# Recurrence: the third job of each inverse made at step 28 for lines 12 to 19, its masks after the final transposes

## The chip, the cores and the metric

The kernel runs on one core of one Trainium2 chip. A core has TensorE (matrix products into PSUM), VectorE, ScalarE, GpSimd (POOL in the profile) and SyncE (SP, which issues the transfers). The metric is the time of one launch on the device, in microseconds. Before the change the median of three runs is 1203.76 us (1202.25 to 1204.63).

## The reference

One layer of a hybrid backbone for 128 context tokens and 512 latent tokens: an adaptive norm, an input projection, an RWKV-7 branch with 8 heads of 64 that runs forward and backward, a neighbourhood-attention branch, a gated merge, and a feed-forward block. The part that matters here is the recurrence of the RWKV branch, for each direction and head:

```python
def _wkv_step(s, inp):
    r, w, k, v, a, b = inp
    sa = jnp.einsum("bhvk,bhk->bhv", s, a)
    s = s * w[:, :, None, :] + sa[..., None] * b[:, :, None, :] + v[..., None] * k[:, :, None, :]
    return s, jnp.einsum("bhvk,bhk->bhv", s, r)

def _wkv_scan(s0, r, w, k, v, a, b, reverse):
    xs = tuple(jnp.moveaxis(t.astype(jnp.float32), 1, 0) for t in (r, w, k, v, a, b))
    s, ys = lax.scan(_wkv_step, s0.astype(jnp.float32), xs, reverse=reverse)
    return s, jnp.moveaxis(ys, 0, 1)
```

Everything is in float32.

## The kernel before, in words

**Chunks and lines.** The kernel does not step through tokens. It cuts the 640 tokens into ten chunks of 64 and treats two heads at a time, so there are four head pairs, `ct` = 0 to 3, one after the other. A chunk in one direction is a *line*; a head pair has 20 lines, 0 to 9 forward and 10 to 19 backward. Lines 0 to 7 and 12 to 19 belong to the 512 latent tokens, lines 8 to 11 to the 128 context tokens. Within a line the rule "state times a, plus b" makes the 64 tokens depend on each other through a triangular matrix, which has to be inverted; after that the lines are chained by products of 64x64 blocks.

**The stages of a head pair.** `main` makes the triangular matrices N of all lines on TensorE and copies them to `Nt`. `inv` inverts them. `carry` walks the state through the lines, eight steps, and makes the outputs. `out` normalises the outputs of the pair and runs woven into the next pair's `inv`; `prep` makes the operands of the next pair and runs woven into `carry`.

**The inverse.** `inv` transposes `Nt` into `RL` on VectorE (line 1218), with the 32x32 diagonal blocks of all lines side by side, and eliminates in 30 steps `s` = 1 to 30 (lines 1235, 1242, or the pairs of 1249 and 1253), all on VectorE, each step reading the one before. Then come the two final transposes on VectorE, RT (line 1262) and T (line 1264). The off-diagonal 32x32 blocks follow by two groups of 80 small products on TensorE: line 1273 reads RT, its result goes to `Hs` by ScalarE (1278), and line 1287 reads T and `Hs`. The finished inverse is `Rt`: eight copies from T on VectorE (1281), and four copies of the second group's result, two on ScalarE and two on VectorE (1292). `carry` reads `Rt` for the first time in line 1348, and `AG` in line 1321 a little before.

**Jobs and masks.** While VectorE eliminates, TensorE has time, and `inv` puts three *jobs* there, each for a range of lines (`parts8`). A job is `v_job` (lines 0 to 9 only: moves the values to the other half of the partitions and copies them to `ZV` by ScalarE, 1172 and 1178), `t_job` (transposes, 1195, copied to `TG` by ScalarE, 1198) and `g_job`: the products of 1144 and 1147 into three PSUM tiles, and, for lines from 10 up, `flip` (1184), which takes the values of line 19 - l from `ZV` in reversed order. So a backward line needs its forward partner's values in `ZV` first. `g_job` returns a function, the *masks*: four VectorE multiplications (two of 1156 into `AG`, two of 1159 into `TG`) that take the products out of PSUM and zero what lies on the wrong side of the diagonal. `PRM["jobs"]` names the steps of the jobs and `PRM["mds"]` those of the masks, per head pair. Before the change the jobs stand at steps 2, 9 and 16 (2, 11 and 16 in pair 3), for lines 0 to 7, 12 to 19 and 8 to 11, and their masks at steps 4, 11 and 19 (4, 13 and 19).

**PSUM.** Jobs, groups and carry all take PSUM tiles from one rotation of six, tag `w`. A job over lines 12 to 19 takes six of them, and the three of its products are held until its masks are done.

**Order of the work.** The order on TensorE, VectorE, ScalarE and GpSimd is the program's order, written out by hand. `weave` runs a stage's generator and, at each of its yields, pulls a number of *fills* from `fill`, the stream of projection matmuls (128x128 times 128x320, line 196) of the rest of the layer; one entry of `PRM["plan"]` gives the number. Evacuations of the projections, such as the shifts of lines 520 to 523 and the merges of line 1461 (pair 3), are put behind a set number of fills, on ScalarE and VectorE. The plan has ten fills behind each of steps 2, 9 and 16, mostly two behind other steps, and 5, 24 and 20 behind steps 29, 30 and the final transposes in pairs 0 and 1 (18 instead of 20 in pair 2), so that line 1273 stands behind them on TensorE; pair 3 has six behind most steps from 15 on and 11 behind the transposes. The transfers of the weights are issued by SP in the stream's own order. When the fills from the activations `h` end, in pair 3's inverse, the space of `h` is taken over by the attention and recurrence outputs `o`, loaded back from DRAM.

After the four pairs come the merge, the output projection and the feed-forward block, bound by TensorE throughout.

Of the kernel before, what the change touches and what calls it, by code (L numbers as in the profile page):

```python
# [26 lines left out]
PRM = dict(  # L27
    order=("l0 l1 k0 r0 v0 l2 g0 g1 g2 k1 g3 r1 g4 g5 v1 g6 g7 k2 r2 g8 g9 v2 g10 g11 k3 r3 g12 g13 v3 g15 g14 a0 a1 a2 a3 a4 a5 a6 a7 "
     "b0 b1 b2 b4 b3 b5 b6 b7"),
    plan=(  # L30
        "22.0 0.0 2.0 4.0",
        ("0.0.0 2.0.0 2.0.1 10.0.0 2.0.0 2.0.1 2.0.1 2.0.1 2.0.1 2.0.1 10.0.0 2.0.0 2.0.0 10.0.0 2.0.0 2.0.0 "
         "2.0.0 10.0.0 2.0.0 2.0.0 2.0.0 2.0.0 2.0.0 2.0.0 2.0.0 2.0.0 2.0.0 2.0.0 2.0.0 2.0.0 5.0.0 24.0.0 "
         "20.0.0 10.0.0 8.0.0 8.0.0 0.0.0"),
        ("10.0 1.0 12.1 0.2 0.0 8.1 6.2 0.0 8.1 6.2 0.0 8.1 12.2 0.0 8.1 6.2 0.0 8.1 6.2 0.0 7.1 5.2 0.0 9.1 "
# [32 lines left out]
        "w >hb >lb",  # L68
        ""),
    fp=(6, 12, 18), h2e="dpddddpddd", x0e="a", ze="aa", y2=1, y1=0, sc=3, sr=3, sp=1, mg=1.915, h1=0.952,  # L70
    h2=0.91, jobs=((2, 9, 16), (2, 9, 16), (2, 9, 16), (2, 11, 16)),
    mds=((4, 11, 19), (4, 11, 19), (4, 11, 19), (4, 13, 19)), bud=((1.8, 0.8), (1.3, 1.8)), off=6, tk=2, h3=1,
    h4=1.07, g1=2, km="dddddddd", kb="ddpd", ma="d", yo="pppp", r0="pd", rl=(0, 0, 0), lh=(0, 0, 1, 1),
    wl="dddddddddppppppppppppppppppppppppppdpppppppppppp", nu=9, na=(
        "6.0.12.0.1 6.0.12.0.0 6.0.12.0.0 6.0.12.0.2 6.0.12.0.0 6.0.12.0.2 6.0.12.0.0 6.0.12.0.2 6.0.12.0.0 "
        "6.0.12.0.2 6.0.12.1.0 6.1.12.1.2 6.2.12.2.0 6.1.12.2.2 6.0.12.2.0 6.1.12.1.2 6.2.14.2.0 "
        "6.2.14.1.2 6.2.14.2.0 6.2.14.2.0 6.3.18.2.0 10.0.10.0.0"))
# [24 lines left out]
def V(ap, dims, off=0):  # L102

    return bass.AP(ap.tensor, ap.offset + off, [list(ap.ap[0])] + [list(d) for d in dims])
# [3 lines left out]
def body(ctx: ExitStack, tc: tile.TileContext, xs, xp, cols, consts, w_ada, b_row, w_rw, w_qkv,  # L108
# [366 lines left out]
    pend, off, hold = [], [0], [False]  # L475
# [557 lines left out]
    with ExitStack() as s3:  # L1033
# [76 lines left out]
        parts8 = ((0, 8), (12, 20), (8, 12))  # L1110
# [102 lines left out]

        def inv(ct, S):

            jobs, mds = dict(zip(PRM["jobs"][ct], parts8)), PRM["mds"][ct]
            RL = nk_t("RL", [P, 40, 32])[:, :32, :]
            dve.transpose(RL, V(Nt[:, 0, :], [[20, 32], [1, 32]]))

# [5 lines left out]
            masks = []  # L1225
# [36 lines left out]
            dve.transpose(RT, V(RL[:, 0, :], [[1, 32], [32, 32]]))  # L1262
            T = V(f5()[:, :], [[32, 32], [1, 32]])
            dve.transpose(T, RL)
            Hs = nk_t("Hs", [P, 40, 32])
            lohi = [(slice(64 * h, 64 * h + 32), slice(64 * h + 32, 64 * h + 64)) for h in range(2)]
            yield 2
# [223 lines left out]
        with tc.manual_schedule(engines=FIRST):  # L1491
# [4 lines left out]
            for ct in range(4):  # L1496
# [8 lines left out]
                if ct < 3:  # L1505
                    prep_dma(ct + 1, S2, sb.tile([P, NT], F32, tag="mx", bufs=2, name=nm("upw")))
                weave(inv(ct, S), (og, bg))
                drain(og)
                marks.add(f"I{ct}")
# [486 lines left out]
```

## Time and profile before

| what | value |
|---|---|
| median of three runs | 1203.76 us (1202.25 to 1204.63) |
| the profiled execution | 1201.55 us |
| its span, first to last instruction | 1199.8 us |
| mean granted TensorE clock | 0.985 |
| the four pairs' recurrence, about | 262 to 680 us |
| TensorE busy in 262 to 680 us | 381.8 of 418 us |
| VectorE busy in 262 to 680 us | 281.1 of 418 us |

The inverses stand at about 266 to 314, 366 to 420, 470 to 522 and 576 to 638 us of the span, each with the groups behind it. How to read the rows that follow: a row of the timeline is start, duration, engine, line, operation, output and inputs by the program's names, shapes and count, and in brackets the time that the engine sat idle before it and what released it. Several instructions of one line are merged into one row. A row of the chain has start, duration, engine, output and line. PE is TensorE, DVE is VectorE, ACT is ScalarE. Busy time of TensorE includes modelled ends, so a gap shows in the bracket rather than in the share.

### The profile page before, as it was taken

To read this page: it belongs to the slowest core of one execution; us is meant where nothing else is said; L and a number is where in the kernel's file an instruction comes from. 1 tells how busy PE (TensorE), PEld (TensorE's weight loads), DVE (VectorE), ACT (ScalarE), POOL (GpSimd) and SP (SyncE) were. 2 spreads that over 40 slices of the span, in tenths; PEclk is the share of its full clock that TensorE was granted. 3 is DMA by queue.
4 is the path that set the end of the run, shared out by engine and by line. 5 is a ranking of instruction groups with operands and counts; after the bars stand their busy time and mean duration, and the time that the engine had idled before them with its cause. 6 is when DMAs were issued, how large, how long until landed. Compare 5 with 4: busy or idle time off the path is not lost.

```text
span 1199.8 us, 26920 instructions
## 1 busy us (share of the span) xinstructions
PE 1128.0 (94%) x11160; PEld 999.2 (83%) x11160; DVE 793.3 (66%) x1630; ACT 503.6 (42%) x1016; POOL 273.8 (23%) x354
## 2 busy tenths in 40 slices
PE   6999999998998899899789989989999999999998
PEld 4588877788887788788778878889889989998997
DVE  4565455569558838946594684888568756875675
ACT  4444666653454364346323331754224412442240
POOL 1162244343224323342231360200001000000000
PEclk9999999999899999999899989999999999999999
DMA  9752777531211221120432571312312231222122
GB/s 336 245 115 88 238 219 231 197 124 48 66 48 37 83 69 49 54 87 29 164 129 87 177 272 54 105 36 89 106 53 88 89 105 53 89 90 90 67 73 104
DMA packets 56578, 134.48 MB, mean 112 GB/s; under 512 B 7140, under 2 KB 22116, under 8 KB 56456
## 3 DMA queue, kind: packets, MB, share of 16 engines
q1 hardware_dynamic: 55592, 131.56, 33.1%
q8 instruction: 88, 1.44, 0.5%
q10 hardware_dynamic: 864, 1.20, 0.3%
q14 instruction: 34, 0.28, 0.1%
HBM read 118.41 MB, written 14.32 MB: 111 GB/s over the span
## 4 chain that ended last, share of the span: by engine, by line
PE 61%; DVE 11%; issue 2%; ACT 2%; DMA 1%; SPq 0%; POOL 0%; DVEq 0%; ACTq 0%
PE f L1715 23%; PE acc L283 16%; PE fl L196 10%; DVE pr L1249 2%; DVE RL L1253 2%; PE w L1361 1%; PE w L1321 1%; DVE AG L1104 1%; PE w L1333 1%; PE w L1348 1%; PE mm L196 1%; PE w L1147 1%; DMA tr<-trw_d 1%; PE w L1378 1%; DVE f L1262 1%
## 5 line engine op out<-in xcount | busy, mean ns | idle before, releaser
L196 PE MATMUL fl<-h,whi 128*128 128x320 f32 x704 | 170.4, 323 | 1.9 <-ACT U L515 1.0
L175 POOL TENSOR_TENSOR wlo<-wst,whi 128x256 fp32r<-128x256 f32 x118 | 102.8, 899 | 192.1 <-ACT whi L170 188.7
L1715 PE MATMUL f<-t,whi 128*128 128x320 f32 x640 | 141.4, 309 | 0.0
L1715 PE MATMUL f<-b,whi 128*128 128x320 f32 x608 | 136.4, 312 | 3.6 <-ACT b L185 1.8
L283 PE MATMUL acc<-whi,u 128*128 128x512 f32 (+1 forms) x448 | 135.9, 385 | 0.0
L196 PEld LDWEIGHTS fl<-h,whi 128*128 128x128 f32 x704 | 121.1, 192 | 6.8 <-ACT U L515 1.2
L170 ACT CAST whi<-wst 128x1024 fp32r<-128x1024 f32 (+2 forms) x86 | 81.8, 956 | 83.2 <-PE acc L283 32.9
L196 PE MATMUL fl<-h,wlo 128*128 128x320 f32 x352 | 114.6, 326 | 0.0
L1715 PEld LDWEIGHTS f<-t,whi 128*128 128x128 f32 x640 | 107.0, 188 | 0.0
L1715 PEld LDWEIGHTS f<-b,whi 128*128 128x128 f32 x608 | 102.8, 190 | 4.7 <-ACT b L185 2.2
L1770 POOL TENSOR_TENSOR ws<-wst 128x512 f32<-128x512 f32 x20 | 27.4, 1372 | 342.0 <-DVE wlo L1759 226.2
L1715 PE MATMUL f<-t,wlo 128*128 128x320 f32 x320 | 98.9, 309 | 0.0
L283 PEld LDWEIGHTS acc<-whi,u 128*128 128x128 f32 x448 | 83.5, 188 | 16.6
L1715 PE MATMUL f<-b,wlo 128*128 128x320 f32 x304 | 94.6, 311 | 1.4 <-DVE wlo L1759 1.4
L1756 ACT CAST whi<-ws 128x1024 fp32r<-128x1024 f32 x40 | 42.0, 1050 | 108.7 <-PE f L1715 48.5
L283 PE MATMUL acc<-wlo,u 128*128 128x512 f32 (+1 forms) x224 | 86.3, 385 | 0.0
L175 DVE TENSOR_TENSOR wlo<-wst,whi 128x1024 fp32r<-128x1024 f32 (+1 forms) x49 | 61.6, 1267 | 36.5 <-ACT whi L170 36.0
L283 PE MATMUL acc<-whi,h 128*128 128x512 f32 x240 | 78.7, 402 | 1.4 <-DVE h L397 1.4
L196 PEld LDWEIGHTS fl<-h,wlo 128*128 128x128 f32 x352 | 67.8, 193 | 2.6
L1555 DVE SCALAR_TENSOR_TENSOR tt<-acc,G 128x512 f32<-128x512 f32 (+1 forms) x51 | 34.7, 681 | 51.0 <-PE acc L283 51.0
L196 PE MATMUL mm<-h,whi 128*128 128x320 f32 x288 | 65.5, 315 | 0.0
L196 PE MATMUL fl<-o,whi 128*128 128x320 f32 x224 | 56.3, 331 | 7.1 <-DMA o<-o_d 4.8
(332 smaller groups left out, 2562.1 us busy)
## 6 DMA issues: line engine op xcount, KB each, us to landing
wst<-in_w_dram SPq DMA_DIRECT2D x66, 512.0 KB
wst<-in_w_rw_dram SPq DMA_DIRECT2D x31, 512.0 KB
wa<-in_w_ada_dram SPq DMA_DIRECT2D x24, 512.0 KB
f<-in_w_ada_dram SPq DMA_DIRECT2D x16, 512.0 KB
wst<-in_w_qkv_dram SPq DMA_DIRECT2D x12, 512.0 KB
o<-o_d SPq DMA_DIRECT2D x14, 320.0 KB
x<-in_xs_dram SPq DMA_DIRECT2D x8, 512.0 KB
wa<-in_w_ada_dram SPq DMA_DIRECT2D x16, 256.0 KB
```

The costliest lines, as they stand in the source:

```text
L170: act.copy(hi[:, :n], st[:, :n])
L175: eng.tensor_tensor(out=lo[:, a:b], in0=st[:, a:b], in1=hi[:, a:b].bitcast(F32), op=ALU.subtract)
L196: pe.matmul(ps[:, :t1 - t0], w[:, a:a + 128], x[:, k0 + kt, t0:t1], start=n == 0, stop=n == 3 * nk - 1)
L283: pe.matmul(pss[i][:, a:b], lhs(x, kt, ts_), w[:, cs_], start=ki == 0 and n == 0, stop=ki == last and n == 2)
L1104: dve.tensor_tensor(out=AG[rr, c, h, :], in0=c64(S.kk[rr, :], d), in1=S.P65[d][rr, :, 0:64], op=ALU.mult)
L1147: pe.matmul(pr[h][hrows[h ^ i], o_], x[hrows[h], :], R_[hrows[h], l, :], start=True, stop=True)
L1249: dve.tensor_tensor(out=prv, in0=V(RL[:, s + 1 + a, :], [[32, b - a], [0, s]], s), in1=V(RL[:, s, :], [[0, b - a], [1, s]]), op=ALU.mult)
L1253: dve.tensor_tensor(out=dst, in0=dst, in1=prv, op=ALU.add)
L1555: dve.scalar_tensor_tensor(out=tt, in0=ps[:, a:b], scalar=c, in1=G[:, g, sl], op0=ALU.mult, op1=ALU.mult)
L1715: pe.matmul(ps[:, :H2], w_[:, c_], x_[:, kt, :], start=first and kt + n == 0, stop=last and kt == 3 and n == 2, skip_group_check=more)
L1756: act.copy(r[0][:, :width], src())
L1770: eng_x(PRM["se"][i - 1]).tensor_tensor(out=o_, in0=x, in1=y, op=op)
```

## The change

The jobs now stand at steps 2, 9 and 28 (2, 11 and 28 in pair 3). A new parameter `jo` gives their order: the first job is for lines 8 to 11, the second for lines 0 to 7, the third for lines 12 to 19. The masks of the first two follow at steps 4 and 12 (4 and 14); those of the third are made after the two final transposes, ahead of the copies into `Rt`. The numbers of fills in the plan stay as they are.

```diff
-    h2=0.91, jobs=((2, 9, 16), (2, 9, 16), (2, 9, 16), (2, 11, 16)),
-    mds=((4, 11, 19), (4, 11, 19), (4, 11, 19), (4, 13, 19)), bud=((1.8, 0.8), (1.3, 1.8)), off=6, tk=2, h3=1,
+    h2=0.91, jobs=((2, 9, 28), (2, 9, 28), (2, 9, 28), (2, 11, 28)),
+    mds=((4, 12), (4, 12), (4, 12), (4, 14)), bud=((1.8, 0.8), (1.3, 1.8)), off=6, tk=2, h3=1,
...
-    wl="dddddddddppppppppppppppppppppppppppdpppppppppppp", nu=9, na=(
+    wl="dddddddddppppppppppppppppppppppppppdpppppppppppp", nu=9, jo=(2, 0, 1), na=(
...
         def inv(ct, S):
 
-            jobs, mds = dict(zip(PRM["jobs"][ct], parts8)), PRM["mds"][ct]
+            jobs, mds = dict(zip(PRM["jobs"][ct], (parts8[i] for i in PRM["jo"]))), PRM["mds"][ct]
...
             T = V(f5()[:, :], [[32, 32], [1, 32]])
             dve.transpose(T, RL)
+            for f in masks:
+                f()
             Hs = nk_t("Hs", [P, 40, 32])
```

## The prediction

> **What bounds the kernel now.** I read the page first, then the chain that ended last, then the rows of the four inverses by engine. The page gives each engine's busy time and share, and the chain's shares by engine.
>
> ```profile
> PE 1128.0 (94%) x11160; PEld 999.2 (83%) x11160; DVE 793.3 (66%) x1630; ACT 503.6 (42%) x1016; POOL 273.8 (23%) x354
> PE 61%; DVE 11%; issue 2%; ACT 2%; DMA 1%; SPq 0%; POOL 0%; DVEq 0%; ACTq 0%
> ```
>
> TensorE sets the end; the change adds and drops no matmul, so only an idle stretch of TensorE can be won or lost. VectorE holds 11% of the chain, and the chain in order of time (start, duration, work) shows where: at the ends of the inverses. I number these 0 to 3, as `ct`.
>
> ```profile
> 300.27 1.91 DVE f L1262
> 302.32 1.48 PE w L1273 x72
> 303.81 4.34 PE fl L196 x18
> ...
> 309.40 2.83 PE fl L196 x18
> ...
> 410.25 4.06 PE fl L196 x18
> ...
> 512.28 4.08 PE fl L196 x17
> ```
>
> L1262 is the first of the two final transposes (RT), L1273 the matmul group that reads it, L196 the filler projections. TensorE's rows at the group, with the idle time and its releaser in brackets, inverses 0 to 3:
>
> ```profile
> 302.32 1.48 PE L1273 MATMUL w<-f,Nt 32*32 32x32 f32 x80 [5.33 <-DVE f L1262]
> 408.75 1.49 PE L1273 MATMUL w<-f,Nt 32*32 32x32 f32 x80 [3.30 <-DVE f L1262]
> 510.80 1.48 PE L1273 MATMUL w<-f,Nt 32*32 32x32 f32 x80 [3.66 <-DVE f L1262]
> 627.94 1.47 PE L1273 MATMUL w<-f,Nt 32*32 32x32 f32 x80 [0.25 <-DVE f L1262]
> ```
>
> In inverses 0 to 2 TensorE has run out of filler and stands 12.3 us in all for VectorE's elimination. In inverse 3 the two arrive together. After the idles the same 18 fills take 4.34 and 4.06 us where 2.83 is the pace (17: 4.08 against 2.67): 1.51, 1.23 and 1.41 us more, the price of a TensorE that slows after standing.
>
> **The change part by part.** (1) Masks. VectorE's rows of inverse 0 show what a set of masks costs in its queue: from its first row to the elimination step behind it.
>
> ```profile
> 280.53 1.39 DVE L1156 TENSOR_TENSOR AG<-w,K 64x512 f32<-64x512 f32 x2
> ...
> 283.04 0.57 DVE L1249 TENSOR_TENSOR pr<-RL 128x108 f32<-128x108 f32 x2
> ...
> 289.39 0.86 DVE L1156 TENSOR_TENSOR AG<-w,K 64x256 f32<-64x256 f32 x2
> ...
> 290.83 1.42 DVE L1249 TENSOR_TENSOR pr<-RL 128x100 f32<-128x100 f32 x2
> ```
>
> Eight lines cost 283.04 - 280.53 = 2.51 us, four lines 290.83 - 289.39 = 1.44. Ahead of RT stood 2.51 + 2.51 + 1.44; now 1.44 (at step 4) + 2.51 (at step 12 or 14). RT comes 2.51 us earlier in each inverse, and TensorE's idle ahead of L1273 shrinks by as much.
>
> (2) What the moved masks are ahead of now: VectorE's copies into Rt (L1281, L1292) and the shifts of the projections. VectorE's total is unchanged, so these copies end when they ended before, not earlier. The carry's first group that reads Rt is L1348. Rows of the copies and of L1348, inverses 0 to 3:
>
> ```profile
> 305.35 3.60 DVE L1281 COPY Rt<-f 32x320 f32<-32x320 f32 x8
> 309.88 0.89 DVE L1292 COPY Rt<-w 32x320 f32<-32x320 f32 x2 [0.94 <-ACT Rt L1292]
> 313.73 0.68 PE L1348 MATMUL w<-x,Rt 64*64 64x64 f32 x16
> 416.05 0.89 DVE L1292 COPY Rt<-w 32x320 f32<-32x320 f32 x2 [0.56 <-ACT Rt L1292]
> 419.48 0.68 PE L1348 MATMUL w<-x,Rt 64*64 64x64 f32 x16
> 519.28 0.89 DVE L1292 COPY Rt<-w 32x320 f32<-32x320 f32 x2
> 521.53 0.68 PE L1348 MATMUL w<-x,Rt 64*64 64x64 f32 x16
> 633.69 0.89 DVE L1292 COPY Rt<-w 32x320 f32<-32x320 f32 x2 [0.26 <-ACT Rt L1292]
> 636.31 0.68 PE L1348 MATMUL w<-x,Rt 64*64 64x64 f32 x16
> ```
>
> From the end of L1292 to L1348 there are 313.73 - 310.77 = 2.96 us, then 2.54, 1.36 and 1.73. This slack, plus whatever VectorE waits vanish, is the most that an inverse can give: once RT is early, Rt is late next, and I expect L1348 to wait for L1292. The masks themselves are needed only by L1321 and later, and are ready some microseconds before it.
>
> (3) Jobs on TensorE. Inverse 1 shows the lengths: first row of a job to the first fill behind it, for lines 0 to 7, 12 to 19 and 8 to 11.
>
> ```profile
> 364.47 0.97 PE L1172 MATMUL w<-K,vp 64*64 64x64 f32 x26
> ...
> 369.73 0.42 PE L196 MATMUL fl<-h,whi 128*128 128x320 f32 x1
> ...
> 376.52 1.16 PE L1195 MATMUL w<-K,f 64*64 64x64 f32 x64
> ...
> 380.45 0.27 PE L1147 MATMUL w<-R__2889,f 64*64 64x64 f32 x2 [1.15 <-issue]
> ...
> 380.95 0.56 PE L196 MATMUL fl<-h,whi 128*128 128x320 f32 x2
> ...
> 385.66 0.27 PE L1172 MATMUL w<-K,vp 64*64 64x64 f32 x2
> ...
> 388.00 0.42 PE L196 MATMUL fl<-h,wlo 128*128 128x320 f32 x1
> ```
>
> That is 5.26, 4.43 and 2.34 us. Now step 2 is 5.26 - 2.34 = 2.92 us shorter, step 16 loses 2.34, step 28 gets 4.43; TensorE's arrival at L1273 moves by -2.92 - 2.34 + 4.43 = -0.83, or by up to +4.43 if the early savings are swallowed by other waits. Between the job at step 28 and L1273 stand 2 + 5 + 24 + 20 = 51 fills of the plan (2.83 / 18 x 51 = 8.0 us), so its results are long ready when the masks want them; inverse 3 has 29 (6 + 6 + 6 + 11). No DMA moves: SP and POOL queues keep their order.
>
> Rows where one engine waits for the other inside inverses 1, 2 and 3:
>
> ```profile
> 369.73 1.39 DVE L1156 TENSOR_TENSOR AG<-w,K 64x512 f32<-64x512 f32 x2 [0.41 <-PE w L1144]
> 380.95 1.39 DVE L1156 TENSOR_TENSOR AG<-w,K 64x512 f32<-64x512 f32 x2 [1.45 <-PE w L1144]
> 481.59 0.49 DVE L1095 TENSOR_TENSOR bv<-w,vp 128x320 f32<-128x320 f32 x1 [2.04 <-PE w L1093]
> 583.88 1.39 DVE L1156 TENSOR_TENSOR AG<-w,K 64x512 f32<-64x512 f32 x2 [2.81 <-PE w L1144]
> 592.40 0.90 PE L196 MATMUL fl<-o,whi 128*128 128x320 f32 x2 [4.78 <-DMA o<-o_d]
> 616.62 0.56 PE L196 MATMUL fl<-o,whi 128*128 128x320 f32 x2 [1.44 <-DVE mt L1461]
> ```
>
> In the first half VectorE waits for TensorE, so a first job 2.92 us shorter passes on; these waits can shrink or vanish. (4) Not shown before: at step 2 the flips of lines 10 and 11 now wait on TensorE for ScalarE's copies of ZV (L1178).
>
> ```profile
> L1178 ACT COPY ZV<-w 64x512 f32<-64x512 f32 (+1 forms) x32 | 13.5, 421 | 15.5 <-PE w L1184 7.0 <-PE w L1172 6.0 <-PE w L1144 2.2
> ```
>
> Between 0 and two copies, 0.84 us; I take 0 in inverses 0 to 2, where the idle at L1273 covers it, and without that cover it costs the 0.84.
>
> **The sum**, as the time by which L1348 comes earlier. Inverse 0: at least 2.51 (part 1; TensorE still slow), at most slack 2.96 + L1292's own 0.94 = 3.90; I take the middle, 3.2. Inverse 1: 2.51 to 2.54 + 0.56 + 0.41 + 1.45 = 4.96; middle, 3.8 (idle 3.30 plus part of the 1.23). Inverse 2: 1.36 (slack alone) to 1.36 + 2.04 = 3.40; middle, 2.4. Inverse 3 has no idle to close: TensorE moves by -0.83 and loses the 1.44 that stood behind masks, so up to 2.27 + 0.25 = 2.5; if the transfer of `o` comes no earlier, -2.34 + 4.43 - 1.44 - 0.25 = 0.4 late. I take 1.5, nearer the upper end, because that transfer follows the last fill in TensorE's order. Together 3.2 + 3.8 + 2.4 + 1.5 = 10.9 us, ends 2.51 + 2.51 + 1.36 - 0.4 = 6.0 and 3.90 + 4.96 + 3.40 + 2.5 = 14.8. The profiled execution took 1201.55 us (span 1199.8, 1.75 around it), so 1190.7 there; the median of the runs is 2.2 higher, 1203.76 - 10.9 = **1192.9 us**, ends 1189.0 and 1197.8. What follows the inverses is the same work, started earlier.
>
> The Trainium skill, "TensorE: Matmul & The Clock Gate", Part 1, says that about 3.4 us of idleness halve TensorE's clock until it has been busy as long again. The rows agree roughly: 5.33, 3.30 and 3.66 are followed by slow fills, 0.25 is not. By that rule the idles left (2.8 at most) keep the clock, inverse 0 goes to its 3.90, and the sum is 11.6; if 2.8 still slows, inverse 0 stays at 2.51 and the sum is 10.2.
>
> **The rivals.** (A) TensorE becomes the bound: the first job's 2.92 us are swallowed, and it arrives 4.43 - 2.34 = 2.09 later. Then 5.33 leaves the full 2.51, the others give 3.30 - 2.09 = 1.21, 1.36 and 0.25 - 2.09 = -1.84: 3.2 us, 1200.5. For it: the third job stands late, and each long job shows about 1.15 us of issue idle. Against: the early waits are VectorE's, not TensorE's. The skill's "Runtime: NRT & Kernel Launch", Instruction fetch mechanics, calls crossing a 16 KiB block of instructions mostly hidden; the 1.15 us in mid-job do not look hidden, and if they were at step 28, A would give back up to 1.15 us in inverses 1 and 3 each.
>
> (B) Slower: the same lateness grown to the whole job, because step 16's saving is swallowed too: TensorE is kept back by evacuations that hang on VectorE (such as the 1.44 row) and then meets 4.43 us of job. The inverses give 5.33 - 4.43 = 0.90, -1.13, -0.77 and -4.18: 5.2 us later, 1208.9. It decides from a lateness of about 3.1 us, where 2.23 + 0.20 + 0.56 - 2.85 is about 0. Against it: inverse 0 shows TensorE idle only at the end.
>
> (C) The saving is handed back on VectorE: it waits at step 12 as long as it gained, so RT is not earlier, and the copies of Rt, 2.51 us later, run past the slack in inverses 2 and 3 (1.15 + 0.78): 1205.7. For it is the 1.45 row; against it, that inverse 0 has no such wait.
>
> **How the numbers follow.** Forecast, 1189.0 to 1197.8: 0.65; more than its upper gain: 0.03; A, up to about 1201.5: 0.18; B 0.08; C 0.06. The range 1188.5 to 1201.0 leaves out B, C and little of A, under 2 in 10. 0.2% is 2.4 us, about what a measurement of this kernel tells from no change. Faster: 0.65 + 0.03 + 0.16 of A = 0.84; same: 0.02 of A + 0.05 of C = 0.07; slower: B and 0.01 of C = 0.09.
>
> **What would show it.** Right: the idle before L1273 falls to under 3 us in inverse 0 and near 1 or less in 1 and 2; the 18 fills behind it take under 3 us in 1 and 2; L1348 gets a new, short wait for L1292; the AG rows lose their 0.41 and 2.81. Wrong: L1273 follows fills without idle and later than now (A, B), or AG at step 12 shows new waits of 2 us (C), or L1348 waits more than 1.5 us for Rt.

## The result, and the profile after

| | median, us | range of the runs | ratio to before, with its 95% interval |
|---|---|---|---|
| before, in the same rounds | 1203.62 | 1200.61 to 1204.63 | |
| the changed kernel | 1197.93 | 1196.17 to 1203.88 | 0.9958 [0.9940, 0.9975] |
| the changed kernel once more (e1_again) | 1200.21 | 1197.19 to 1204.16 | 0.9973 [0.9960, 0.9987] |

By the ratios the change makes the kernel faster, by 5.1 us in the first set of runs and 3.3 us in the second. That is the forecast's direction, inside its range, and less than half of its 10.9 us. The profiled executions alone would mislead: the one of before (1201.55 us) lies under its median, the one of after (1203.88 us, span 1202.1) is the slowest of its runs. Stages therefore have to be compared, and several profiles.

In the changed kernel the line numbers from 1264 on are higher by two (L1273 is L1275, L1281 is L1283, L1292 is L1294, L1348 is L1350, L1461 is L1463). The page's busy times and the chain's shares by engine:

```profile
PE 1134.1 (94%) x11160; PEld 1006.9 (84%) x11160; DVE 799.6 (67%) x1630; ACT 503.6 (42%) x1016; POOL 271.8 (23%) x354
PE 58%; DVE 15%; DMA 2%; ACT 2%; issue 2%; SPq 0%; POOL 0%; DVEq 0%; ACTq 0%
```

The same instructions take 6 us more on VectorE (793.3 before) and 6 us more on TensorE (1128.0), and VectorE's share of the chain grew from 11% to 15%. So VectorE was not relieved: something made its instructions longer.

The starts of the four inverses (L1218), of RT (L1262) and of the groups L1275 and L1350 in the changed kernel, from the timelines of VectorE and TensorE:

```profile
267.91 1.25 DVE L1218 STREAM_TRANSPOSE RL<-Nt 128x1024 f32<-128x1024 f32 x1 [1.47 <-issue]
302.36 1.90 DVE L1262 STREAM_TRANSPOSE f<-RL 128x1024 f32<-128x1024 f32 x1
304.40 1.49 PE L1275 MATMUL w<-f,Nt 32*32 32x32 f32 x80 [5.82 <-DVE f L1262]
315.95 0.68 PE L1350 MATMUL w<-x,Rt 64*64 64x64 f32 x16
367.82 1.25 DVE L1218 STREAM_TRANSPOSE RL<-Nt 128x1024 f32<-128x1024 f32 x1 [2.37 <-ACT Nt L1130]
403.41 2.04 DVE L1262 STREAM_TRANSPOSE f<-RL 128x1024 f32<-128x1024 f32 x1
405.59 1.46 PE L1275 MATMUL w<-f,Nt 32*32 32x32 f32 x80 [0.82 <-DVE f L1262]
416.37 0.96 PE L1350 MATMUL w<-x,Rt 64*64 64x64 f32 x14 [0.98 <-DVE Rt L1294]
466.94 1.25 DVE L1218 STREAM_TRANSPOSE RL<-Nt 128x1024 f32<-128x1024 f32 x1 [3.08 <-ACT Nt L1130]
504.44 2.10 DVE L1262 STREAM_TRANSPOSE f<-RL 128x1024 f32<-128x1024 f32 x1
507.73 1.47 PE L1275 MATMUL w<-f,Nt 32*32 32x32 f32 x80
518.59 0.96 PE L1350 MATMUL w<-x,Rt 64*64 64x64 f32 x14 [1.04 <-DVE Rt L1294]
572.87 1.25 DVE L1218 STREAM_TRANSPOSE RL<-Nt 128x1024 f32<-128x1024 f32 x1 [2.75 <-ACT Nt L1130]
625.05 2.08 DVE L1262 STREAM_TRANSPOSE f<-RL 128x1024 f32<-128x1024 f32 x1
638.17 0.68 PE L1350 MATMUL w<-x,Rt 64*64 64x64 f32 x16
```

Before, L1218 started at 266.44, 365.45, 469.53 and 575.54. From L1218 to RT it was 33.83, 41.32, 39.30 and 50.30 us; now it is 34.45, 35.59, 37.50 and 52.18. So RT is 5.73 us earlier in inverse 1 and 1.80 in inverse 2, but 0.62 **later** in inverse 0 and 1.88 later in inverse 3. TensorE still stands 5.82 us in inverse 0 (5.33 before).

**Inverse 0: splits of weights on elimination rows.** GpSimd makes the low halves of the weights (L175, the split: a full weight minus its rounded half, both in SBUF) while VectorE eliminates. VectorE and GpSimd of the changed kernel, then the same stretch before:

```profile
278.18 3.35 POOL L175 TENSOR_TENSOR wlo<-wst,whi 128x256 fp32r<-128x256 f32 x4 [8.22 <-ACT whi L170]
278.69 1.51 DVE L1249 TENSOR_TENSOR pr<-RL 128x99 f32<-128x99 f32 x2
280.13 1.52 DVE L1253 TENSOR_TENSOR RL<-RL,pr 128x99 f32<-128x99 f32 x2
```

```profile
278.28 0.43 DVE L1249 TENSOR_TENSOR pr<-RL 128x99 f32<-128x99 f32 x2
280.38 2.91 POOL L175 TENSOR_TENSOR wlo<-wst,whi 128x256 fp32r<-128x256 f32 x4 [11.89 <-ACT whi L170]
280.53 1.39 DVE L1156 TENSOR_TENSOR AG<-w,K 64x512 f32<-64x512 f32 x2
281.85 1.27 DVE L1159 TENSOR_TENSOR TG<-w,K 128x512 f32<-128x512 f32 x2
```

An elimination row of this size takes 0.43 us alone and 1.5 us beside a split. The masks, which read a product in PSUM and a constant, take 1.39 and 1.27 us beside a split, no more than elsewhere. Before, one of the three splits of inverse 0 lay wholly beside masks and the second for 1.5 of its 4.05 us; three elimination rows took about 1.4 us. Moving the masks away put the splits on the elimination, and now seven rows take 1.0 to 1.5 us. The delay can also fall on GpSimd: that second split (at 288.07, before) took 4.05 us instead of 2.8 to 2.9, and the elimination rows at its start kept their 0.45 us. Summing, over the two-instruction rows of L1249 and L1253, what each takes above the shortest row of its shape in the profile gives an excess of about 3.5 us before and 6.7 after: 3.2 us lost against the 2.51 us of masks saved, and RT is later (0.62 measured, 0.7 by this sum). Over the four inverses the same sum grows from 9.4 to 15.8 us, about the 6 us by which VectorE's busy time grew.

The Trainium skill has a rule for this ("SBUF — State Buffer", "Who interferes with whom"): VectorE and GpSimd share one pair of SBUF ports as an exclusive lock, which a VectorE operation with two SBUF inputs needs when GpSimd reads SBUF. The rows agree, masks with one input in PSUM included; the prediction did not weigh it.

**Inverse 1: more than forecast.** VectorE's waits for TensorE there were 0.41, 0.16, 0.81, 0.48 and 1.45 us before; one of 0.16 is left:

```profile
379.82 1.39 DVE L1156 TENSOR_TENSOR AG<-w,K 64x512 f32<-64x512 f32 x2 [0.16 <-PE w L1144]
```

2.51 us of masks plus 3.15 us of waits are 5.66 of the 5.73 us. The first job, now for four lines, no longer holds VectorE up.

**Inverse 2: the copies are next.** TensorE's waits in the third job, and VectorE's copies into `Rt`:

```profile
495.19 0.33 PE L1147 MATMUL w<-R__2889,f 64*64 64x64 f32 x2 [0.78 <-DVE out L1411]
496.93 0.28 PE L1147 MATMUL w<-R__2889,f 64*64 64x64 f32 x3 [1.42 <-DVE out L1411]
510.21 1.83 DVE L1283 COPY Rt<-f 32x320 f32<-32x320 f32 x4
512.90 2.82 DVE L1283 COPY Rt<-f 32x320 f32<-32x320 f32 x4
513.76 3.71 POOL L175 TENSOR_TENSOR wlo<-wst,whi 128x256 fp32r<-128x256 f32 x4 [6.08 <-ACT whi L170]
```

RT is 1.80 us earlier and not 2.51, since VectorE's waits ahead of it grew from 2.04 to 2.85 us. The third job wants a PSUM tile that the outputs' stage (L1411) still holds, and TensorE reaches L1275 at 507.73, 1.2 us after RT's end at 506.54. The second four copies, 1.82 us before, take 2.82 beside a split, and L1350 waits 1.04 us for VectorE's last copies (L1294). The chain that ended last runs here from RT through T, the third masks, the shifts and the copies to L1350, all on VectorE, so that TensorE's lateness does not set the end of this inverse.

**Inverse 3: slower.** TensorE, VectorE and GpSimd in the changed kernel; then two pieces of its chain that ended last, just ahead of RT (transposes of the job of step 28, and the fills behind that job); then the three engines around the same split before:

```profile
601.38 1.67 DVE L1249 TENSOR_TENSOR pr<-RL 128x112 f32<-128x112 f32 x2
602.15 1.48 POOL L175 TENSOR_TENSOR wlo<-wst,whi 128x256 fp32r<-128x256 f32 x2
602.97 0.99 DVE L1253 TENSOR_TENSOR RL<-RL,pr 128x112 f32<-128x112 f32 x2
607.80 0.90 PE L196 MATMUL fl<-o,whi 128*128 128x320 f32 x2 [5.73 <-DVE mt L1463]
624.65 0.49 DVE L1463 SCALAR_TENSOR_TENSOR P<-mx,fl 128x320 f32<-128x320 f32 x1 [3.35 <-PE fl L196]
631.33 0.56 PE L196 MATMUL fl<-o,whi 128*128 128x320 f32 x2 [1.50 <-DVE P L1463]
```

```profile
619.85 1.09 PE w L1195 x64
...
622.80 1.82 PE fl L196 x11
```

```profile
606.63 1.39 DVE L1156 TENSOR_TENSOR AG<-w,K 64x512 f32<-64x512 f32 x2
607.28 1.41 POOL L175 TENSOR_TENSOR wlo<-wst,whi 128x256 fp32r<-128x256 f32 x2
607.95 1.27 DVE L1159 TENSOR_TENSOR TG<-w,K 128x512 f32<-128x512 f32 x2
609.14 0.46 DVE L1249 TENSOR_TENSOR pr<-RL 128x112 f32<-128x112 f32 x2
611.21 0.56 PE L196 MATMUL fl<-o,whi 128*128 128x320 f32 x2 [0.28 <-DVE mt L1461]
```

The fills here need a merge (L1463) on VectorE for a free PSUM tile. Before, TensorE had the job of step 16 while VectorE was behind, and waited 0.28, then 1.44 and 0.59 us. Now that job is gone and TensorE stands 5.73 us; the wide job comes at step 28, where VectorE, one merge ahead of RT, waits 3.35 us for a fill behind it; and the third masks stand ahead of merges, for which TensorE waits 1.50 and 0.55 us. The split falls on elimination rows and not beside masks, and the excess of this inverse goes from 0.4 to 3.2 us. L1350 starts 65.30 us after L1218, 60.77 before.

### The profile page after: what moved, and what is told of

It is laid out like the page before. It is cut to its first block, busy times and chain, and to the rows that moved or that the text cites. A ratio compares the mean times of both kernels' runs of the same rounds, so it can differ in the third digit from the quotient of the medians.

```text
span 1202.1 us, 26930 instructions
## 1 busy us (share of the span) xinstructions
PE 1134.1 (94%) x11160; PEld 1006.9 (84%) x11160; DVE 799.6 (67%) x1630; ACT 503.6 (42%) x1016; POOL 271.8 (23%) x354
## 3 DMA queue, kind: packets, MB, share of 16 engines
q8 instruction: 88, 1.44, 0.5%
## 4 chain that ended last, share of the span: by engine, by line
PE 58%; DVE 15%; DMA 2%; ACT 2%; issue 2%; SPq 0%; POOL 0%; DVEq 0%; ACTq 0%
PE f L1717 21%; PE acc L283 16%; PE fl L196 10%; DVE pr L1249 2%; DVE RL L1253 2%; PE w L1363 1%; PE w L1323 1%; PE w L1350 1%; DVE AG L1156 1%; PE w L1335 1%; PE mm L196 1%; DVE TG L1159 1%; DVE Rt L1283 1%; DVE AG L1104 1%; DMA tr<-trw_d 1%
## 5 line engine op out<-in xcount | busy, mean ns | idle before, releaser
L175 POOL TENSOR_TENSOR wlo<-wst,whi 128x256 fp32r<-128x256 f32 x118 | 100.7, 882 | 203.2 <-ACT whi L170 199.8
L175 DVE TENSOR_TENSOR wlo<-wst,whi 128x1024 fp32r<-128x1024 f32 (+1 forms) x49 | 60.6, 1243 | 35.3 <-ACT whi L170 34.8
L196 PE MATMUL fl<-o,whi 128*128 128x320 f32 x224 | 58.9, 342 | 13.7 <-DVE mt L1463 5.7
```

The source lines that it names most:

```text
L175: eng.tensor_tensor(out=lo[:, a:b], in0=st[:, a:b], in1=hi[:, a:b].bitcast(F32), op=ALU.subtract)
L196: pe.matmul(ps[:, :t1 - t0], w[:, a:a + 128], x[:, k0 + kt, t0:t1], start=n == 0, stop=n == 3 * nk - 1)
```

## The experiments

Edits are shown against the changed kernel. For experiments, `jo` is given per pair; pairs that are called old have jobs, masks and order of before.

**The noise (e1_again).** The changed kernel, unaltered.

> The changed kernel unaltered, a second profiled execution. Theory 'fixed': what the first profile shows is how the kernel runs each time, so inverse 3 again has a wait of TensorE for L1463 of 5 us or more, inverse 0 again has about seven elimination rows of 1.0 to 1.5 us beside GpSimd's splits, and L1275 of inverse 2 again comes after fills without idle; time about 0.4% under before. Rival 'unlucky execution': one of these is gone, and its span is 5 us or more under the first profile's 1202.1.

Measured: 1200.21 us, 0.9973 [0.9960, 0.9987]. The waits named above are the same in its profile: 5.83 us ahead of L1275 in inverse 0, 5.72 for the merge in inverse 3. They belong to the kernel, not to one execution.

**Pair by pair (e2, e3, e4).**

```diff
e2_pair3_old (pair 3 old; e3: pairs 0 to 2 old; e4: pairs 0 and 3 old)
-    jobs=((2, 9, 28), (2, 9, 28), (2, 9, 28), (2, 11, 28)),
-    mds=((4, 12), (4, 12), (4, 12), (4, 14)), jo=(2, 0, 1)
+    jobs=((2, 9, 28), (2, 9, 28), (2, 9, 28), (2, 11, 16)),
+    mds=((4, 12), (4, 12), (4, 12), (4, 13, 19)), jo=((2, 0, 1), (2, 0, 1), (2, 0, 1), (0, 1, 2))
```

> Changed kernel, but pair 3 keeps the jobs, order and mask steps of before. Theory 'cover': the job at step 16 of inverse 3 was what TensorE did while VectorE was behind with the merges; with it back, the wait of 5.7 us for L1463 falls to 1.5 or less, and the time is 3 to 6 us under the changed kernel. Rival 'port' (inverse 3 lost only by GpSimd's splits falling on elimination steps): 1 to 3 us under it, with the wait for L1463 still above 3 us.

> Kernel before, with pair 3 alone changed. Theory 'cover': 2 to 5 us slower than before, with TensorE waiting over 4 us for L1463 near step 16. Rival 'prediction' (inverse 3 wins 1.5 us): 1.5 us faster than before.

> Pairs 1 and 2 changed, pairs 0 and 3 as before. Theory 'port' for inverse 0 (it gains nothing since the splits of GpSimd now fall on elimination steps): as fast as the kernel with pair 3 alone as before, within 1 us, and inverse 1 shows 4 to 5.5 us less from L1218 to L1348, inverse 2 under 1 us less. Rival (inverse 0 gains its 2.5 to 3.9 us in most executions): 2.5 us or more slower than the kernel with pair 3 alone as before.

> The kernel of e2_pair3_old unaltered (pairs 0, 1 and 2 new, pair 3 as before the change), beside e10 to e12 in the same rounds. Nothing is left out. Both theories: 0.993 to 0.995 of the time before, GpSimd's splits in inverse 0 on rows of 1.0 to 1.5 us again, 6.8 us of excess.

Measured: e2 0.9934 [0.9920, 0.9947] and, run again as e9, 0.9947 [0.9928, 0.9965]; e3 1.0036 [1.0020, 1.0053]; e4 0.9947 [0.9935, 0.9959]. In e3 TensorE waits 5.72 us for the merge; in e2 the wait is

```profile
609.48 0.57 PE L196 MATMUL fl<-o,whi 128*128 128x320 f32 x2 [1.43 <-DVE mt L1463]
```

Pairs 1 and 2 give 6.4 us (0.0053 x 1204), pair 0 at most 1.6 (e4 against e2; nothing against e9), and pair 3 costs 4.3 us by e3 (1.3 to 4.7 by the two sets of the changed kernel against e2 and e9). Stage by stage, in us, from L1218 to the next L1218, and in pair 3 from L1218 to L1350:

| profile | pair 0 | pair 1 | pair 2 | pair 3 |
|---|---|---|---|---|
| before | 99.01 | 104.08 | 106.01 | 60.77 |
| e3 (pairs 0 to 2 old) | 99.05 | 106.22 | 106.90 | 64.61 |
| after | 99.91 | 99.12 | 105.93 | 65.30 |
| e1 | 100.11 | 99.31 | 108.03 | 64.21 |
| e2 (pair 3 old) | 99.53 | 99.07 | 104.40 | 60.65 |
| e9 (pair 3 old) | 99.31 | 99.12 | 105.77 | 60.95 |
| e4 (pairs 0, 3 old) | 100.34 | 99.75 | 104.36 | 62.27 |
| e10 (all old, three splits of pair 0 moved, see below) | 100.18 | 109.84 | 104.34 | 59.69 |

The gain is pair 1's. Pair 0 gives nothing. In pair 2 the old form took 104.34 to 106.90 us and the new one 104.36 to 108.03, so no gain is shown there. Pair 3 takes about 3.6 us: 64.7 in the mean of three profiles of the new form, 61.1 in the mean of ten of the old one (e5, e6, e8, e11 and e12 below also have it).

**The place of the third masks (e6_masks30)**, pair 3 old:

```diff
-    mds=((4, 12), (4, 12), (4, 12), (4, 13, 19))
+    mds=((4, 12, 30), (4, 12, 30), (4, 12, 30), (4, 13, 19))
```

> The changed kernel's form for pairs 0, 1 and 2, but with the masks of the third job at step 30, so ahead of the final transposes instead of behind them; pair 3 as before the change. Nothing is left out. To be held against e2_pair3_old. Theory, the gain of pairs 1 and 2 comes from where the last masks stand: they wait for a job made two steps ahead (2.5 us of products) and take 1.4 to 2.5 us, so RT of each inverse starts about 2 to 4 us later than in e2, the kernel loses 3 to 6 us against e2 (ratio 0.996 to 0.999), and pair 0 loses 2 at most since its later inverse has slack on nothing. Rival, the gain comes from the order of the jobs (the wide ones first) and the end of step 16's job alone: the time stays within 1 us of e2 (0.993).

Measured: 1200.20 us, 0.9970 [0.9949, 0.9991], by the ratios 4.3 us more than e2 and 2.8 more than e9. RT starts 36.96, 37.58 and 38.60 us after L1218, 2.50, 2.11 and 2.13 later than in e2 (2.49, 2.12 and 1.15 later than in e9), and TensorE stands again:

```profile
304.96 1.48 PE L1275 MATMUL w<-f,Nt 32*32 32x32 f32 x80 [8.31 <-DVE f L1262]
408.48 1.46 PE L1275 MATMUL w<-f,Nt 32*32 32x32 f32 x80 [3.43 <-DVE f L1262]
510.14 1.48 PE L1275 MATMUL w<-f,Nt 32*32 32x32 f32 x80 [1.11 <-DVE f L1262]
```

So the core of the change does what it says: masks ahead of RT delay RT, by about their own length except in inverse 2 against e9. In time the loss is clear of e2's interval; e9's overlaps.

**The PSUM tile (e5_job30)**, pair 3 old:

```diff
-    jobs=((2, 9, 28), (2, 9, 28), (2, 9, 28), (2, 11, 16))
+    jobs=((2, 9, 30), (2, 9, 30), (2, 9, 30), (2, 11, 16))
```

> The changed kernel's form for pairs 0, 1 and 2 with the third job two steps later (step 30 instead of 28), pair 3 as before the change; nothing is left out. To be held against e2_pair3_old, the same kernel with step 28 (0.9934 of the time before). Theory, a PSUM tile: the job waits until the product of L1411 has given back its PSUM tile (0.78 and 1.42 us in pair 2, 1.99 in pair 1), and two steps later seven of the fills stand ahead of it, so that TensorE works through the wait: the waits for L1411 shrink by about 1 us in pair 2, the fills there end about 1 us earlier, and the kernel gains 0.5 to 1 us on e2 (0.993). Rival, the wait is for VectorE as a whole and moves with the job: the waits stay at 2 us together and the time is that of e2, or up to 1 us more since fewer steps are left to cover the job.

Measured: 1196.99 us, 0.9944 [0.9927, 0.9961], no gain on e2 and e9. On TensorE, L1275 of inverse 2 comes earlier, 38.49 us after L1218 against 40.17 in e2, although the waits for L1411 shrank there only from 2.38 to 2.06 us. It was then lost on VectorE:

```profile
510.57 3.68 DVE L1283 COPY Rt<-f 32x320 f32<-32x320 f32 x4
517.10 1.30 PE L1350 MATMUL w<-x,Rt 64*64 64x64 f32 x14 [2.82 <-DVE Rt L1294]
```

A split on GpSimd (510.49, 3.48 us) lies on the four copies, which take 3.68 us instead of 1.82, and L1350 waits 2.82 us. In inverse 2 the copies of `Rt` are the next bound, and a split beside them sets their length.

**Splits off GpSimd in inverse 0 (e8, e10, e11).** A letter of `wl` names the engine of each split; three of inverse 0 move to VectorE, one instruction of 128x1024 each.

```diff
e8_split_dve, e11_split_dve_again (pair 3 old); e10_before_split_dve (all pairs old)
-    wl="dddddddddppppppppppppppppppppppppppdpppppppppppp"
+    wl="dddddddddppdddpppppppppppppppppppppdpppppppppppp"
```

> The kernel of e2_pair3_old with one other edit: the three splits of weights (L175) that GpSimd makes in inverse 0 while VectorE eliminates are made by VectorE, one instruction of 128x1024 each. Nothing is left out, and every other engine's order stays. Theory, the splits on GpSimd slow the elimination steps that they fall on (rows of 1.0 to 1.5 us instead of 0.35 to 0.46, 6.8 us of excess in inverse 0): the excess falls under 1.5 us, three rows of about 1.25 us come in on VectorE, RT of inverse 0 starts about 3 us earlier, and the kernel is 2 to 3 us faster than e2 (0.991). Rival, the slowed rows have another cause (their operands, or waits that the rows hold): the excess stays, VectorE gets 3.8 us more work, RT of inverse 0 is 3 to 4 us later and the kernel 2 to 4 us slower than e2 (0.996).

> The kernel before in all four pairs, with GpSimd's three splits of inverse 0 made by VectorE as in e8_split_dve; nothing is left out. With e8, e9 and the kernel before it makes a square of two edits. Theory, in the old order half of GpSimd's split time lies beside the masks at no cost and the excess is only 3.5 us, so that taking it away and adding three rows of 1.23 us cancel: RT of inverse 0 stays at 33.5 to 34.5 us after L1218 (33.83 before), the time stays within 2 us of before (0.998 to 1.002), and against e8's 30.18 the change's own saving in inverse 0, hidden in the changed kernel, shows as 3.5 to 4 us, near the forecast's 3.2. Rival, the move of the splits is worth the same in either order: RT comes 3 to 4 us earlier here too (30 to 31), the kernel gains 2 to 3 us (0.998), and the change itself gives inverse 0 nothing even without GpSimd.

> The kernel of e8_split_dve unaltered, in the same rounds as e9. Nothing is left out. Its trace had inverse 0 ending 3.4 us earlier than in e2_pair3_old, but its times spread over 10 us and its median was no lower. Theory, the earlier RT of inverse 0 is on the path that sets the end: 2 to 4 us faster than e9 (0.990 to 0.992). Rival, it is handed back further on: the same as e9 within 1 us.

Measured: e8 1195.78 us, 0.9930 [0.9906, 0.9954], alone no proof of a gain; e11 1193.96 us, 0.9923 [0.9908, 0.9938], in the same rounds as e9's 1197.29; e10 1205.81 us, 1.0015 [1.0003, 1.0027]. The start of inverse 0, the first split on VectorE, RT and (e8) the group behind it, in e8 and then in e10:

```profile
265.51 1.25 DVE L1218 STREAM_TRANSPOSE RL<-Nt 128x1024 f32<-128x1024 f32 x1 [1.65 <-issue]
276.98 1.22 DVE L175 TENSOR_TENSOR wlo<-wst,whi 128x1024 fp32r<-128x1024 f32 x1
295.69 1.94 DVE L1262 STREAM_TRANSPOSE f<-RL 128x1024 f32<-128x1024 f32 x1
297.77 1.47 PE L1275 MATMUL w<-f,Nt 32*32 32x32 f32 x80 [1.58 <-DVE f L1262]
```

```profile
266.04 1.25 DVE L1218 STREAM_TRANSPOSE RL<-Nt 128x1024 f32<-128x1024 f32 x1 [1.22 <-issue]
280.80 1.23 DVE L175 TENSOR_TENSOR wlo<-wst,whi 128x1024 fp32r<-128x1024 f32 x1 [1.28 <-ACT whi L170]
301.05 1.91 DVE L1262 STREAM_TRANSPOSE f<-RL 128x1024 f32<-128x1024 f32 x1
```

The excess falls from 6.7 us to 0.2 in e8 and e11, and from 3.5 to 0.2 in e10. L1218 to RT is now a square of two edits:

| inverse 0, L1218 to RT, us | splits on GpSimd | splits on VectorE |
|---|---|---|
| old order | 33.83 | 35.01 |
| new order | 34.45 (after), 34.46 (e2), 34.47 (e9) | 30.18 (e8), 30.17 (e11) |

With the splits out of the way the change is worth 4.8 us in inverse 0. Of that, 1.28 us is e10's wait for a rounded half and 0.92 us a wait of its first masks for TensorE; without both, 2.6 us are left, close to the masks' 2.51. With the splits on GpSimd the change costs 0.6. In the old order moving the splits gains nothing. Each edit alone gains nothing in inverse 0. Together they shorten pair 0's stage from 99.53 and 99.31 us (e2, e9) to 96.18 and 96.19 (e8, e11). In time e11 is 3.3 us faster than e9, though the intervals overlap, and e8 lies within the noise of e2.

Not all of the price of standing went with the idle. Behind e8's 1.58 us TensorE's granted clock is still 0.50 from 299.2 to 302.4 us, and L1350 comes 11.39 us after L1275, as before the change (11.40).

**Two more splits (e12_split_more):** the splits on the eliminations of inverses 1 and 2, shown against e8's line.

```diff
-    wl="dddddddddppdddpppppppppppppppppppppdpppppppppppp"
+    wl="dddddddddppdddppppdppppppdpppppppppdpppppppppppp"
```

> The kernel of e8_split_dve with two more splits of weights moved from GpSimd to VectorE, the one that falls on elimination steps in inverse 1 (6.8 us long in e2) and the one in inverse 2 (5.8 us). Nothing is left out. Theory, they too slow the rows that they fall on: the excess of inverses 1 and 2 falls from 3.3 and 2.8 us to under 1 each, two rows of 1.2 us come in, RT comes 1 to 2 us earlier in each; but TensorE waits for the PSUM tile of L1411 and for Rt there, so no more than 1 to 2 us of it reach the end, 0 to 2 us faster than e11. Rival, the added rows cost what the collisions did: RT within 0.5 us of e11's and the same time.

Measured: 1194.58 us, 0.9926 [0.9911, 0.9941], like e11. The excess falls only to 1.8 and 1.7 us (3.2 and 2.7 in e8), since other splits still overlap, and RT starts 35.98 and 37.52 us after L1218, 35.11 and 36.64 in e11, 35.49 and 36.82 in e8: the added rows cost at least what the collisions did. The rival held in time; RT came up to 0.9 us later, more than its 0.5.

**Pair 3's loss (e7, e13, e14, e15).**

```diff
e7_pair3_order (e13: with the split moved; e15: that and the three splits of inverse 0)
-    jobs[3]=(2, 11, 28), mds[3]=(4, 14)
+    jobs[3]=(2, 11, 16), mds[3]=(4, 14, 19)
e13 and e14_after_split3 (e14: jobs, masks and order as in the changed kernel)
-    wl="dddddddddppppppppppppppppppppppppppdpppppppppppp"
+    wl="dddddddddppppppppppppppppppppppppdpdpppppppppppp"
```

> The changed kernel in pairs 0, 1 and 2; in pair 3 the new order of the jobs (lines 12 to 19 last), but the third job back at step 16 and its masks at 19, so that TensorE has that work where VectorE is late. Nothing is left out. To be held against e2_pair3_old (pair 3 wholly old) and the changed kernel (pair 3 wholly new, 4.5 us slower than e2). Theory, the job at step 16 is cover: TensorE's wait for the merge of L1463, 5.73 us in the changed kernel, is under 1.5 us, L1350 of pair 3 starts within 1 us of e2's 60.65 us after L1218, and the time is e2's within 1 us (0.992 to 0.995). Rival, the order of the jobs or the masks' places are what cost in pair 3: the wait stays above 3 us, or the time is 2 us or more above e2 (0.995 and up).

> The kernel of e7_pair3_order with one split of weights in pair 3 (128x512, beside the elimination rows behind step 13) made by VectorE, two steps later, instead of GpSimd. Nothing is left out. Theory, the second half of pair 3's loss is that collision: the rows of 1.67 and 0.99 us return to 0.46, the masks of step 14 come about 1.7 us earlier, the job's wait of 3.28 us falls to 1.6 or less, and the time is that of e2 and e9 (0.993 to 0.995). Rival, the new order of the jobs itself is later in pair 3: the wait stays near 3 us and the time 0.995 to 0.997.

> The changed kernel in all four pairs with the same one split of pair 3 made by VectorE. Nothing is left out. Theory, both causes add: TensorE's wait for the merge of L1463 in pair 3, 5.73 us, falls by 1.5 to 2 us, not to nothing, since the job that covered it is still at step 28, and the kernel is 1 to 2 us faster than the changed kernel (0.9958 and 0.9973 so far): 0.995 to 0.996. Rivals: the missing job alone sets the wait, which stays over 5 us, and the time stays; or the collision alone does, the wait falls under 2 us, and pair 3 ends like e2's (0.994).

> The kernel of e13 with the three splits of inverse 0 made by VectorE too (e8, e11). Nothing is left out. Theory: the savings add, 0.992 like e11's or up to 1 us better. Rival, pair 3 in the new order stays behind the old: 1 to 3 us slower than e11 (0.993 to 0.995).

Measured: e7 0.9954 [0.9934, 0.9973]; e13 0.9941 [0.9918, 0.9963]; e14 0.9961 [0.9940, 0.9981]; e15 1193.90 us, 0.9926 [0.9905, 0.9947]. These intervals overlap, so the stage has to tell. TensorE's waits for VectorE in pair 3's inverse, in e7, e13 and e14, the longest of each:

```profile
608.15 0.48 PE L1144 MATMUL w<-AG,f 64*64 64x64 f32 x4 [3.28 <-DVE AG L1156]
```

```profile
598.13 0.33 PE L1144 MATMUL w<-AG,f 64*64 64x64 f32 x4 [2.23 <-DVE AG L1156]
```

```profile
603.19 0.90 PE L196 MATMUL fl<-o,whi 128*128 128x320 f32 x2 [4.67 <-DVE mt L1463]
```

| pair 3, us | L1218 to RT | L1275 to L1350 | L1218 to L1350 |
|---|---|---|---|
| old, ten profiles | 49.17 to 51.76 | 8.30 to 8.37 | 59.69 to 62.28 |
| new (after, e1, e3) | 52.18, 51.09, 51.49 | 10.89 in each | 65.30, 64.21, 64.61 |
| e7: job back at 16 | 53.15 | 8.31 | 63.66 |
| e13 (and e15): and the split moved | 51.33 (51.38) | 8.30 (8.33) | 61.83 (61.91) |
| e14: new, split moved | 50.91 | 11.40 | 64.54 |

The loss has two parts. The larger is clear: 2.5 us lie behind the transposes, the length of the late job's masks, which stand ahead of merges and copies there. It is the same in every profile of the new form, and e7 and e13, with those masks at step 19, have the old 8.3 us again. The rest lies ahead of RT and is smaller than the spread of the old form: 51.6 us in the mean of the new form, 50.6 in the old. Ahead of RT 2.51 us of masks are gone there, but the excess beside splits is some 2.8 us higher and the late job makes VectorE wait 3.35 us. Moving the one split brings RT 1.8 us earlier between e7 and e13, but only 0.2 to 1.3 between the new form and e14. That the missing job of step 16 costs time by itself is not shown: with a job back there (e7) TensorE's wait for the merge falls from 5.73 to 1.59 us, and RT is not earlier.

Against the forecasts: e7's L1350 came 3.0 us later than e2's and not within 1 us, since the job itself waits 3.28 us for masks that the split made late. In e13 that wait fell to 2.23 us, not to 1.6, and the time was as forecast. In e14 the wait for the merge fell by 1.06 us, less than the 1.5 to 2 forecast. In the totals, e13 lies with e2 and e9, e14 with the changed kernel. e15 gains nothing on e11, where pair 3 is wholly old.

## Why the prediction was right or wrong

**Right.** The direction; that the masks ahead of RT were the price (e6); that `Rt` would be next: L1350 waits 0.98 and 1.04 us for L1294 in inverses 1 and 2. Inverse 1's idle fell from 3.30 to 0.82 us and inverse 2's from 3.66 to none, the slow fills behind them went (granted clock 1.00 from 405.59 to 413 us), and the waits of 0.41 and 2.81 us on `AG` are gone. Inverse 0 did not give its sign: its idle stayed at 5.82 us where under 3 was forecast. That idles of up to 2.8 us keep the clock is not what the runs show: 1.58 us in e8 did not (0.50 for more than 3 us), and 1.11 in e6 did not either.

**Right in sum by luck, wrong in its split.** Pairs 1 and 2 together gave 6.4 us against 6.2 forecast, but not as 3.8 + 2.4. Inverse 1 gave 5.5 us in the first two profiles (54.03 to 48.55 us from L1218 to the group that reads `Rt`), more than the upper end of 4.96, because every wait of VectorE went and not only those that I added. Inverse 2 gave 0.35 (52.00 to 51.65, again to the rows behind the wait), less than its lower end of 1.36: VectorE's new waits ahead of RT and the longer copies of `Rt`. Other profiles of the new form, read the same way, give from 0.3 us of loss (e1) to 2.5 of gain (e4). The forecast for the copies, that "these copies end when they ended before, not earlier", held nowhere: after L1218 the last of them ends 2.4 us later in inverse 0, 2.6 earlier in inverse 1, 1.4 later in inverse 2 and 4.3 later in inverse 3. It took VectorE's total as unchanged, where the waits shrank and the rows beside splits grew.

**The step that failed first** is part 1: "RT comes 2.51 us earlier in each inverse". It priced the masks and left the elimination rows as they were. But the masks had been a place where GpSimd's splits cost nothing. In inverse 0 that turned 2.5 us saved into 0.6 lost, and the term of 3.2 us into nothing (e8 and e10 show 2.6 to 4.8 where the splits are away). In inverse 3 too RT came 0.8 to 1.9 us later than before the change. The row of 1.42 us that stands behind the masks at 290.83 was quoted in part 1 as their end, without asking why it was three times its neighbours.

**The step that failed by most** is the term for inverse 3. Step 16's 2.34 us were booked as a saving, the 1.44 us wait as one that goes, and the 4.43 us of the wide job at step 28 on TensorE alone, not as something that VectorE waits for; together 1.5 us of gain. In their place the runs show a loss: 3.6 us from L1218 to L1350 in the mean, 4.3 us in time in e3. The wait for the merge grew to 5.7 us in all three profiles, VectorE waited 3.35 us for a fill behind the late job, and the moved masks put their 2.5 us between L1275 and L1350, with no earlier RT to pay for them. Rival B named part of this, TensorE hanging on VectorE's evacuations and then meeting the whole job, and had 4.18 us for inverse 3. That its number fits is partly chance: it had neither the masks' 2.5 us nor the splits, and gave the loss to all four inverses. That TensorE had no idle in inverse 3 was read as nothing to win; it also meant that nothing covers a late VectorE.

The terms 3.2 + (3.8 + 2.4) + 1.5 thus became, in time, 0 to 1.6 + 6.4 - 4.3, or 2.1 to 3.7 us, where the changed kernel itself gave 3.3 and 5.1. The runs of one kernel spread over 2 to 11 us, and e2 and e9, one kernel, differ by 1.6 us; how pair 0 and pair 3 share the difference is not known better than that.

## What to carry to other kernels

Before moving an instruction off a busy engine, look at what runs beside it on the other engines: an instruction beside which another engine's work costs nothing is worth more than its length, and taking it away and taking that work away may pay only together (e11: 0.9923). Before booking a removed job as a saving, ask whether the engine that loses it then waits for something (here 5.73 us instead of 1.44), and who waits for the job where it now stands (3.35 us). And price each stage for itself; the same edit gave more than forecast in one inverse and cost about 4 us in another.

## What the runs showed of the hardware

- A row of two elimination instructions on VectorE (0.43 us) takes 1.5 us beside a GpSimd split of SBUF operands, four copies SBUF to SBUF take up to 3.68 us instead of 1.82, while masks with a PSUM input keep their 1.39 and 1.27 us. The same split takes 1.22 us in one VectorE instruction and 2.8 to 4.1 us in four on GpSimd in inverse 0.
- The stage of pair 1 in its old form, with the same instructions of that pair in the same order, took 104.08, 106.22 and 109.84 us in three profiles (before, e3, e10); in the new form it stays between 98.3 and 101.3. VectorE's waits ahead of RT add up to 3.31, 4.11 and 7.75 us there, and the wait put down to "issue" in the job of step 2 is 1.16 us before and 2.17 in e3 and in e10; what starts these delays is not shown. One profile of before could not show this spread, and it may be why pair 1 gave more than its own profile promised.
- How long TensorE may stand before its clock falls is not one number here. After idles of 1.57 and 1.58 us ahead of L1275 (e8, e11, e12) the granted clock fell to 0.50 and the fills behind were slow; after 1.64 in e10 it did not. After 0.82 us it stayed at 1.00 in the changed kernel and fell in inverse 1 of e8, where L1350 came 11.02 us after L1275 instead of 9.47.
